# Attention's transposes and value sums in runs of two query blocks, and another bank for the eighth merged product

## The chip, the cores and the metric

The kernel runs on one core of a Trainium2 chip. The metric is the device time of one execution in microseconds. TensorE (PE in the profile) multiplies, VectorE (DVE) and ScalarE (ACT) do elementwise work and empty the matmul banks, GpSimd (POOL) and SyncE (SP) mostly issue transfers.

## The reference

A decoder layer on a sequence of 512 tokens of width 1024, in float32. A chunkwise mLSTM (4 heads) and a sliding-window attention with sinks read one normalised input. Their outputs are merged by gates and projected, and a squared-ReLU MLP and a gated per-layer embedding follow. The two parts that matter here:

```python
# attention: 16 query heads, 4 key/value heads of width 64, window 128, query blocks of 128
logits = einsum("bnqhgd,bnkhd->bnhgqk", qb, kb) * 64**-0.5   # masked to the window
m = maximum(max(logits), sink)
pexp = exp(logits - m)
probs = pexp / (sum(pexp) + exp(sink - m))
out = einsum("bnhgqk,bnkhd->bnqhgd", probs, vb)
...
merged = sigmoid(g_a) * (y_a @ w_branch_a) + sigmoid(g_b) * (y_b @ w_branch_b)
x = x + merged @ w_out
```

## The kernel before

Most products split each float32 operand into a high and a low float32r part and sum three matmuls (high-high, high-low, low-high; `pairs`, run by `chain` at L176). Such matmuls fill nearly the whole execution. The kernel is written with a tile framework: a scheduler at compile time puts each engine's instructions into a fixed order, in which an instruction that stands earlier in the text goes first among those that are ready by its own timing. The engines then run their orders and wait for each other by semaphores.

Matmul results go to banks in three rings: `ps_g` (two banks), `ps_t` (two banks) and `ps_a` (two buffers of two banks each, the large ring). After the merges that pool is closed and another takes its place, with a ring `ps_g` of two banks and a ring of three pairs of banks (`pair`).

**Attention.** The 16 units are (kp, n, ab): kp is a pair of key/value heads, n one of four query blocks, ab the head of the pair; each unit has 4 query heads. `swa_probs` makes a unit's scores in a buffer of the large ring (L783, L784), masks them into a scratch tile (a copy L794 on ScalarE and a copy under a mask L795 on VectorE; for block 0 an addition L790), and takes the softmax there (L797 to L810). The scratch tiles come from a ring of four (`tok_scratch`, tag lm); a unit uses half of one.

After both units of a block, `swa_out` transposes their eight probability tiles into another buffer of the large ring (L820), copies them out (L822) into a tile of a ring of two (tag pT), and for n > 0 makes a second copy that is masked by `tri` (L828, same ring). Then it sums over the values by plain float32 matmuls into a bank of `ps_t`, one half of the array for each of the two heads (L841): two pairs of matmuls for block 0, four pairs for the others. The result is split into high and low parts of `yb`, one query head at a time.

The loop over the units works `LOOK` = 2 units ahead and takes one projection from the list `fill` in most turns: the remaining query projections `q_proj` and the mLSTM's `qk_proj`, each 24 matmuls into a bank of `ps_g`. After the loop come `qk_proj(7)`, the mLSTM and `branch_b`, which multiplies `yb`.

**Merging.** `merge(i)`, i = 0 to 7, multiplies `ya` by a slice of `w_branch_a` into a bank of `ps_g`, and VectorE empties that bank by the product with the gate (L1026), then adds the other branch (L1027) and the result is split (tag mg). `merge_sums` makes sums of an even and an odd slice (L1045 to L1048) and splits them (tag ms). `out_proj` follows: its first product `X` takes both banks of the new `ps_g`, in reversed order, and uses the even merges only (`F11`); ScalarE copies `X` to `q1` (L1150) and then `X` is added to by the product with `F12`. Weights are cast to a high part by ScalarE and a low part by VectorE (L137, L138), four buffers of each.

Of the kernel before, what the change touches and what calls it, by code (L numbers as in the profile page):

```python
# [10 lines left out]
F32 = mybir.dt.float32  # L11
# [5 lines left out]
P = 128  # L17
# [3 lines left out]
KT = D // P  # L21
# [15 lines left out]
def block_kernel(  # L37
# [30 lines left out]
    V, A, G, T = nc.vector, nc.scalar, nc.gpsimd, nc.tensor  # L68
# [13 lines left out]
    sp = pool(st_s, "sp", side="right")  # L82
# [4 lines left out]
    def nm(s):  # L87
        n_names[0] += 1
        return f"{s}_{n_names[0]}"


    def ps_g():
        return pp.tile([P, 512], F32, tag="g", bufs=2, name=nm("psg"))

    def ps_t():
        return pp.tile([P, 512], F32, tag="t", bufs=2, name=nm("pst"))
# [15 lines left out]
    def act_hl(n="s"):  # L112
        return [act_r(n), act_r(n)]
# [9 lines left out]
    def tok_scratch(n="lm"):  # L123
        return sp.tile([P, D], F32, tag="lm", bufs=LMB, name=nm(n))
# [9 lines left out]
    def split(dst, src, scale=None):  # L134

        if scale is None:
            A.copy(dst[0], src)  # L137
            last_low[0] = V.tensor_sub(dst[1], src, r32(dst[0]))  # L138
        else:
            done = A.activation(dst[0], src, AF.Copy, scale=scale)  # L140
            V.scalar_tensor_tensor(dst[1], src, scale, r32(dst[0]), ALU.mult, ALU.subtract)
            return done
# [64 lines left out]
    ident = cp.tile([P, P], F32, name="ident")  # L207
# [107 lines left out]
    e1, _ = early_part(1)  # L315
# [75 lines left out]
    with tc.issue_after(copied.ins):  # L391
        xn2, _ = norm(2)
# [3 lines left out]
    for m in range(NT):  # L396
        if m == 1:
            columns(2, xn2)
        elif m == 2:
            with tc.issue_after(on_scalar):  # L400
                xn, _ = norm(3)
            _, on_vector = columns(3, xn)

        ps = ps_g()
        for c in range(3):
            mm_tok(ps[:, :264], wv[c], hT[K3[c]], m, first=c == 0, last=c == 2)
        t = sp.tile([P, 256], F32, tag="vs", bufs=4, name=nm("vs"))
# [57 lines left out]
    for i in range(2):  # L465
        ps = ps_t()
# [305 lines left out]

    yb = [None] * 8
    units = [(kp, n, ab) for kp in range(2) for n in range(NT) for ab in range(2)]
    probs = {}

    def swa_probs(kp, n, ab):
        k0 = max(n - 1, 0) * P
        ls = ps_a()
        for g in range(4):  # L780
            q = qs[kp * 4 + g, ab]
            o = ls[:, g * 256 : (g + 1) * 256]
            T.matmul(o, q[:, n * P : (n + 1) * P], kk[kp][ab][:, k0 : k0 + 256], start=True, stop=False)  # L783
            T.matmul(o, q[:, n * P : (n + 1) * P], kl[kp][ab][:, k0 : k0 + 256], start=False, stop=True)  # L784
        kv = 2 * kp + ab
        sk = sink[:, kv * 4 : kv * 4 + 4]
        ls3 = ls.rearrange("p (g k) -> p g k", g=4)
        lm3 = tok_scratch()[:, :512].rearrange("p (g k) -> p g k", g=4)
        if n == 0:
            V.tensor_tensor(lm3, ls3[:, :, :P], later_key.unsqueeze(1).broadcast_to([P, 4, P]), ALU.add)  # L790
        else:


            A.copy(lm3, ls3[:, :, P:])  # L794
            V.copy_predicated(lm3, later_key.bitcast(mybir.dt.int32).unsqueeze(1).broadcast_to([P, 4, P]), ls3[:, :, :P])  # L795
        mx = small("mx", 4)
        V.tensor_reduce(mx, lm3, AX.X, ALU.max, negate=True)  # L797
        nmx = small("nmx", 4)
        V.scalar_tensor_tensor(nmx, mx, 0.125, nsink[:, kv * 4 : kv * 4 + 4], ALU.mult, ALU.min)  # L799
        ds = small("ds", 4)  # L800
        V.tensor_add(ds, sk, nmx)
        es = small("es", 4)
        A.activation(es, ds, AF.Exp)
        sm = small("sm", 4)
        for g in range(4):
            A.activation(lm3[:, g, :], lm3[:, g, :], AF.Exp, bias=nmx[:, g : g + 1], scale=0.125, accum_out=sm[:, g : g + 1])  # L806
        V.tensor_add(sm, sm, es)
        rc = small("rc", 4)
        V.reciprocal(rc, sm)  # L809
        V.tensor_tensor(lm3, lm3, rc.unsqueeze(2).broadcast_to([P, 4, P]), ALU.mult)  # L810
        probs[kp, n, ab] = lm3

    def swa_out(kp, n):

        lm3 = [probs.pop((kp, n, ab)) for ab in range(2)]
        pt = ps_a()
        for ab in range(2):
            for g in range(4):
                c = ab * 512 + g * P
                T.transpose(pt[:, c : c + P], lm3[ab][:, g, :], ident)  # L820
        pT = sp.tile([P, 1024], F32, tag="pT", bufs=2, name=nm("pT"))
        A.copy(pT, pt)  # L822
        terms = [(vs[max(n - 1, 0)], pT)]
        if n:


            own = sp.tile([P, 1024], F32, tag="pT", bufs=2, name=nm("pT"))
            V.scalar_tensor_tensor(  # L828
                own.rearrange("p (g k) -> p g k", g=8),
                tri.unsqueeze(1).broadcast_to([P, 8, P]),  # L830
                0.0,
                pt.rearrange("p (g k) -> p g k", g=8),
                ALU.is_ge,
                ALU.mult,
            )
            terms.insert(0, (vd[n], own))
        o = ps_t()
        for j, (v, w) in enumerate(terms):
            for ab in range(2):
                c = (2 * kp + ab) * 64  # L840
                T.matmul(o[HALF[ab], :], v[:, c : c + 64], w[:, ab * 512 : (ab + 1) * 512], start=j == 0, stop=j == len(terms) - 1)  # L841
        for g in range(4):
            if n == 0:
                yb[kp * 4 + g] = act_hl("yb")
            split([t[:, n * P : (n + 1) * P] for t in yb[kp * 4 + g]], o[:, g * P : (g + 1) * P])

    nsink = c1.tile([P, 16], F32, name="nsink")
    with tc.issue_after(gate_in.ins):
# [11 lines left out]
    for u in range(16):  # L860
        if u % 3 or u < 3:
            fill.pop(0)()
        if u + LOOK < 16:
            swa_probs(*units[u + LOOK])
        if u % 2:
            swa_out(*units[u][:2])

    ya_parts, ya = big_hl("ya")

# [150 lines left out]
    F11, F12, F22, G1, G2, G3, G4 = ([] for _ in range(7))  # L1020

    def merge(i):
        ps = ps_g()
        mm_T(ps, load_w(w_a[i], KT * P, KT), ya)
        sg = act_f("sga")
        V.tensor_mul(sg, ps, gate_of(gad, i))  # L1026
        V.tensor_add(sg, sg, t2[i])  # L1027
        if i % 2 == 0:
            t = act_r("mg")
            own = [t[:, :256], t[:, 256:]]  # L1030
            split(own, sg[:, 256:])
            F11.append(own)
        else:
            own = act_hl("mg")
            split(own, sg)
            F22.append([q[:, :256] for q in own])
            F12.append([q[:, 256:] for q in own])
        return sg
# [80 lines left out]
    def out_proj():  # L1119

        b11, b12, b21, b22 = b_out
        X = [ps_g(), ps_g()][::-1]
        Y, Z = [[t[:, 0, :], t[:, 1, :]] for t in (pair(), pair())]

        def form(raw):
            return load_w(None, 1024, 2, raw)

        def half(ps, f, w, kh, first, last):
            for t in range(2):
                ops = []  # L1130
                for k in range(2):
                    ops += pairs([h[:, t * P : (t + 1) * P] for h in f[2 * kh + k]], [h[:, k, :] for h in w])
                chain(ps[t], ops, first and kh == 0, last and kh == 1, True)

        def prod(ps, f, b, first, last):
            for kh in range(2):
                half(ps, f, form(b[kh]), kh, first, last)

        def part_of(r, c, t):
            return xk[t + (2 if r == 1 else 0)][:, (c - 1) * 512 : c * 512]  # L1140

        def acc(ps, r, c):
            for t in range(2):
                o = part_of(r, c, t)
                V.tensor_add(o, ps[t], o)

        prod(X, F11, b11, True, False)
        q1 = [act_f("q1") for _ in range(2)]
        for t in range(2):
            copied = A.copy(q1[t], X[t])  # L1150
        with tc.issue_after(copied.ins):
            later()
        for r, c in ((2, 1), (2, 2), (1, 2)):
            for t in range(2):
                nc.gpsimd.dma_start(out=part_of(r, c, t), in_=q1[t], accum_op=ALU.add)
        for kh in range(2):
            V.tensor_add(b11[kh], b12[kh], b11[kh])
        prod(X, F12, b21, False, True)
        acc(X, 1, 1)
        with tc.issue_after(last_mm[0].ins):  # L1160
            prod(Z, G2, b11, True, False)
        acc(Z, 2, 1)
        prod(Y, G3, b12, True, False)
        acc(Y, 2, 2)
        for kh in range(2):
            V.tensor_sub(b21[kh], b21[kh], b11[kh])
            V.tensor_sub(b11[kh], b22[kh], b11[kh])
        prod(Z, G1, b11, False, False)
        acc(Z, 2, 2)
        prod(Y, F22, b21, False, True)  # L1170
        acc(Y, 2, 1)
        half(Z, G4, form(b22[0]), 0, False, False)
        two_columns_of(x1, 0, gmlp)
        two_columns_of(x1, 2, gmlp)
        half(Z, G4, form(b22[1]), 1, False, True)
        acc(Z, 1, 2)
# [386 lines left out]
```

## Time and profile before

| | us |
|---|---|
| median of 3 runs | 873.77 (873.5 to 874.34) |
| the profiled execution | 873.36 |
| its span, first to last instruction | 871.3 |
| TensorE busy with matmuls | 860.2 |
| VectorE busy | 664.8 |
| ScalarE busy | 497.0 |
| attention, first scores to first `branch_b` | 222.3 to 327.6 |

Times in the profile are counted from the start of the span. In a row of the timeline stand the start, the duration (merged rows: from the first start to the last end), the engine, the source line, the operation, the tile that is written and those that are read, the shapes, the count, and in brackets the idle time of the engine before the row and what ended it. Matmuls are pipelined: their durations overlap, and the distance from one start to the next is what each costs. In a row of the waits stand the waiting engine, tile and line, the one waited for, and the sum, the count and the longest wait. In a row of the windows stand the stretch and its length, then the busy times of PE, weight loads (PEld), DVE, ACT and POOL with counts, the granted clock of TensorE, the share of DMA and GB/s.

### The profile page before, as it was taken

The numbers are of one execution on the slowest core, as the hardware profiler recorded it, in microseconds if no ns is written. First come the engines' busy times: TensorE is split into PE (matmuls) and PEld (weight loads), VectorE is DVE, ScalarE is ACT, GpSimd is POOL, SyncE is SP. The second block draws the span as 40 slices with busy tenths as digits, with TensorE's granted clock in tenths as the row PEclk, the third lists the DMA queues.
The fourth block names the chain that finished last, engine by engine and source line by source line (L and its number), as shares of the span: only waits on it lengthen the run. The fifth ranks groups of instructions, "written<-read, shape, count | busy, mean of one in ns | idle before, by whom it ended". The sixth has DMA issues, their size and how long they took to land.

```text
span 871.3 us, 11752 instructions
## 1 busy us (share of the span) xinstructions
PE 860.2 (99%) x4422; PEld 724.9 (83%) x4422; DVE 664.8 (76%) x978; ACT 497.0 (57%) x845; POOL 51.1 (6%) x81
## 2 busy tenths in 40 slices
PE   9999999999999999999999999999999999999996
PEld 7888789999877768888878888888888888888886
DVE  7898978774698889767896669746965795688657
ACT  6776657554676667863343565345535533564743
POOL 3221111000000000000020000000000000002000
PEclk9999999999999999999999999999999999999998
DMA  8677235435121256665243711530262044206502
GB/s 299 200 193 278 97 122 206 160 135 201 50 97 43 80 199 214 219 237 191 78 72 129 258 49 37 206 121 25 75 215 97 1 142 173 73 25 135 180 1 97
DMA packets 36234, 117.76 MB, mean 135 GB/s; under 512 B 5069, under 2 KB 5069, under 8 KB 36178
## 3 DMA queue, kind: packets, MB, share of 16 engines
q1 hardware_dynamic: 28578, 95.77, 31.4%
q0 software_dynamic: 7456, 20.98, 8.7%
q8 instruction: 34, 0.56, 0.2%
q10 hardware_dynamic: 144, 0.26, 0.1%
q14 instruction: 22, 0.18, 0.1%
HBM read 99.17 MB, written 11.54 MB: 127 GB/s over the span
## 4 chain that ended last, share of the span: by engine, by line
PE 92%; DVE 3%; ACT 2%; issue 1%; DMA 1%; SPq 0%; DVEq 0%; ACTq 0%
PE psg L176 49%; PE psp L176 23%; PE psa L176 10%; PE pst L176 3%; PE pst L841 1%; PE psp L1111 1%; DMA xt<-in_x 1%; ACT lm L806 1%; ACT wh L137 1%; PE psa L783 1%; PE psa L923 1%; PE psa L945 1%; PE psa L943 1%; PE psa L944 1%; PE psa L784 1%
## 5 line engine op out<-in xcount | busy, mean ns | idle before, releaser
L137 ACT CAST wh<-wr 128x1024 fp32r<-128x1024 f32 x129 | 135.8, 1053 | 157.2 <-PE psg L176 61.0
L138 DVE TENSOR_TENSOR wl<-wr,wh 128x1024 fp32r<-128x1024 f32 x129 | 157.3, 1221 | 82.8 <-ACT wh L137 80.5
L176 PE MATMUL psg<-x,wh 128*128 128x512 f32 x512 | 157.7, 390 | 0.0
L176 PE MATMUL psp<-wh,uf 128*128 128x512 f32 x448 | 138.7, 389 | 0.0
L176 PEld LDWEIGHTS psg<-x,wh 128*128 128x128 f32 x512 | 96.1, 188 | 19.8
L176 PE MATMUL psg<-x,wl 128*128 128x512 f32 x256 | 99.7, 389 | 0.0
L176 PEld LDWEIGHTS psp<-wh,uf 128*128 128x128 f32 x448 | 84.1, 188 | 17.3
L176 PE MATMUL psp<-wl,uf 128*128 128x512 f32 x224 | 87.2, 389 | 0.0
L176 PE MATMUL psg<-h,wh 128*128 128x512 f32 x256 | 81.0, 395 | 0.7 <-DVE rc L809 0.7
L137 ACT CAST wh<-wd 128x1024 fp32r<-128x1024 f32 x44 | 46.2, 1052 | 54.2 <-PE psp L176 21.9
L138 DVE TENSOR_TENSOR wl<-wd,wh 128x1024 fp32r<-128x1024 f32 x44 | 53.2, 1220 | 14.6 <-ACT wh L137 14.5
L176 PEld LDWEIGHTS psg<-x,wl 128*128 128x128 f32 x256 | 48.1, 188 | 10.0
L176 PEld LDWEIGHTS psg<-h,wh 128*128 128x128 f32 x256 | 46.9, 188 | 11.1 <-issue 1.6
L176 PE MATMUL psg<-h,wl 128*128 128x512 f32 x128 | 50.6, 395 | 0.0
L138 DVE TENSOR_TENSOR uf<-F,uf 128x1792 fp32r<-128x1792 f32 (+2 forms) x20 | 33.0, 1652 | 21.8 <-ACT uf L137 21.8
L176 PEld LDWEIGHTS psp<-wl,uf 128*128 128x128 f32 x224 | 42.1, 188 | 8.9
L176 PE MATMUL psg<-yb,wh 128*128 128x512 f32 x128 | 40.2, 393 | 0.0
L1279 DVE SCALAR_TENSOR_TENSOR xk<-psp,r,xk 128x512 f32<-128x512 f32 x48 | 33.8, 746 | 8.0 <-PE psp L176 7.7
L176 PE MATMUL psg<-ya,wh 128*128 128x512 f32 x128 | 39.8, 391 | 0.0
L137 ACT CAST uf<-F 128x1792 fp32r<-128x1792 f32 (+2 forms) x20 | 27.9, 1395 | 20.5 <-DVE F L1255 20.4
L806 ACT ACTIVATE lm<-lm,nmx 128x128 f32<-128x128 f32 x64 | 24.9, 391 | 12.2 <-DVE nmx L799 12.2
L176 PEld LDWEIGHTS psg<-h,wl 128*128 128x128 f32 x128 | 24.0, 188 | 9.0 <-issue 4.1
(365 smaller groups left out, 1854.9 us busy)
## 6 DMA issues: line engine op xcount, KB each, us to landing
wr<-in_w_up SPq DMA_DIRECT2D x32, 512.0 KB, 3.3
wd<-in_w_down SPq DMA_DIRECT2D x24, 512.0 KB, 3.9
wr<-in_w_qsw SPq DMA_DIRECT2D x8, 512.0 KB, 4.3
gd<-gr POOLq DMA_DIRECT2D x8, 512.0 KB, 3.6
wr<-in_w_qkml SPq DMA_DIRECT2D x8, 512.0 KB, 3.2
wr<-in_w_b SPq DMA_DIRECT2D x8, 512.0 KB, 3.2
wh<-in_w_b POOLq DMA_DIRECT2D x8, 512.0 KB, 3.7
gl<-gd SPq DMA_DIRECT2D x8, 512.0 KB, 3.3
```

What stands on the lines that cost most here:

```text
L137: A.copy(dst[0], src)
L138: last_low[0] = V.tensor_sub(dst[1], src, r32(dst[0]))
L176: last_mm[0] = T.matmul(ps, l, r, start=first and i == 0, stop=last and i == len(ops) - 1, skip_group_check=parts)
L783: T.matmul(o, q[:, n * P : (n + 1) * P], kk[kp][ab][:, k0 : k0 + 256], start=True, stop=False)
L784: T.matmul(o, q[:, n * P : (n + 1) * P], kl[kp][ab][:, k0 : k0 + 256], start=False, stop=True)
L806: A.activation(lm3[:, g, :], lm3[:, g, :], AF.Exp, bias=nmx[:, g : g + 1], scale=0.125, accum_out=sm[:, g : g + 1])
L841: T.matmul(o[HALF[ab], :], v[:, c : c + 64], w[:, ab * 512 : (ab + 1) * 512], start=j == 0, stop=j == len(terms) - 1)
L923: T.matmul(psc[s], l, r, start=j == 0, stop=j == 2, skip_group_check=True)
L943: T.matmul(o, hi, vm[s][:, h, :], start=s == 0, stop=False, skip_group_check=True)
L944: T.matmul(o[:, :DV], hi, low[:, s, :], start=False, stop=False, skip_group_check=True)
L945: last_mm[0] = T.matmul(o, lo, vm[s][:, h, :], start=False, stop=s == t, skip_group_check=True)
L1279: V.scalar_tensor_tensor(o, ps[:, t, :], r2[:, 2 * toks + t : 2 * toks + t + 1], o, ALU.mult, ALU.add)
```

## The change

In attention, the two units of a block now write the two halves of one scratch tile. `swa_out` runs after every fourth unit, for two query blocks: `swa_turn` transposes a block and copies the transposes back into that same tile, and makes the masked copy as before, for both blocks; then `swa_sum` makes the value sums of both, the later block first; then both are split. The tiles of tag pT now hold the masked copies alone. The eighth merge writes a bank of `ps_t` instead of `ps_g`, and `out_proj` takes its two banks for `X` in the order of the ring.

```diff
+        if ab == 0:
+            block[kp, n] = tok_scratch()
-        lm3 = tok_scratch()[:, :512].rearrange("p (g k) -> p g k", g=4)
+        lm3 = block[kp, n][:, ab * 512 : (ab + 1) * 512].rearrange("p (g k) -> p g k", g=4)
...
-    def swa_out(kp, n):
-        lm3 = [probs.pop((kp, n, ab)) for ab in range(2)]
+    def swa_turn(kp, n):
+        pT = block.pop((kp, n))
         pt = ps_a()
-        for ab in range(2):
-            for g in range(4):
-                c = ab * 512 + g * P
-                T.transpose(pt[:, c : c + P], lm3[ab][:, g, :], ident)
-        pT = sp.tile([P, 1024], F32, tag="pT", bufs=2, name=nm("pT"))
+        for c in range(0, 1024, P):
+            T.transpose(pt[:, c : c + P], pT[:, c : c + P], ident)
         A.copy(pT, pt)
...
+        return terms
+
+    def swa_out(kp, ns):
+        terms = {n: swa_turn(kp, n) for n in ns}
+        sums = {n: swa_sum(kp, terms[n]) for n in reversed(ns)}
+        for n in ns:
+            for g in range(4):
+                if n == 0:
+                    yb[kp * 4 + g] = act_hl("yb")
+                split([t[:, n * P : (n + 1) * P] for t in yb[kp * 4 + g]], sums[n][:, g * P : (g + 1) * P])
+
+    def swa_sum(kp, terms):
         o = ps_t()
         for j, (v, w) in enumerate(terms):
             for ab in range(2):
                 c = (2 * kp + ab) * 64
                 T.matmul(o[HALF[ab], :], v[:, c : c + 64], w[:, ab * 512 : (ab + 1) * 512], start=j == 0, stop=j == len(terms) - 1)
+        return o
...
-        if u % 2:
-            swa_out(*units[u][:2])
+        if u % 4 == 3:
+            kp, n, _ = units[u]
+            swa_out(kp, (n - 1, n))
...
     def merge(i):
-        ps = ps_g()
+        ps = ps_t() if i == KT - 1 else ps_g()
...
-        X = [ps_g(), ps_g()][::-1]
+        X = [ps_g(), ps_g()]
```

More of the change, by code (lines that the diff above doesn't have):

```diff
@@ L774, in block_kernel @@
     units = [(kp, n, ab) for kp in range(2) for n in range(NT) for ab in range(2)]
-    probs = {}
+    block = {}
     def swa_probs(kp, n, ab):
@@ L810, in swa_probs @@
         V.tensor_tensor(lm3, lm3, rc.unsqueeze(2).broadcast_to([P, 4, P]), ALU.mult)
-        probs[kp, n, ab] = lm3
-    def swa_out(kp, n):
-        lm3 = [probs.pop((kp, n, ab)) for ab in range(2)]
+    def swa_turn(kp, n):
+        pT = block.pop((kp, n))
         pt = ps_a()
-        for ab in range(2):
-            for g in range(4):
-                c = ab * 512 + g * P
-                T.transpose(pt[:, c : c + P], lm3[ab][:, g, :], ident)
-        pT = sp.tile([P, 1024], F32, tag="pT", bufs=2, name=nm("pT"))
+        for c in range(0, 1024, P):
+            T.transpose(pt[:, c : c + P], pT[:, c : c + P], ident)
         A.copy(pT, pt)
@@ L841, in swa_out @@
                 T.matmul(o[HALF[ab], :], v[:, c : c + 64], w[:, ab * 512 : (ab + 1) * 512], start=j == 0, stop=j == len(terms) - 1)
[L842 to L845, printed above, removed]
+        return o
     nsink = c1.tile([P, 16], F32, name="nsink")
```

## The prediction

> **What bounds the kernel now.** I read the page first (span, busy shares, chain), then the waits of TensorE's matmul queue, then the two stages that the change touches in order of time.
>
> ```profile
> span 871.3 us, 11752 instructions
> PE 860.2 (99%) x4422; PEld 724.9 (83%) x4422; DVE 664.8 (76%) x978; ACT 497.0 (57%) x845; POOL 51.1 (6%) x81
> PE 92%; DVE 3%; ACT 2%; issue 1%; DMA 1%; SPq 0%; DVEq 0%; ACTq 0%
> PE psg L176 <- DVE sga L1026: 0.9, 1, 0.9
> PE psg L176 <- DVE rc L809: 0.7, 1, 0.7
> PE psa L783 <- DVE lm L795: 0.5, 1, 0.5
> PE pst L841 <- ACT pT L822: 0.2, 1, 0.2
> 222.00:327.60 105.60, 104.33 (x540) 79.05 (x539) 87.86 (x192) 71.03 (x232) 1.59 (x3) 1.00 0.28 94
> ```
>
> TensorE is busy 99% of the span and is 92% of the chain. In the list of its waits these four are all after the start of the kernel. Three lie in attention, which runs from 222 to 327.6 us with 104.33 of 105.60 us busy (last row, first busy column; the last 1.00 before the DMA share is the granted clock). So the time falls only by what TensorE no longer waits, or no longer spends between instructions.
>
> **Part 1: joining runs of value sums (L841).** A value sum is a plain float32 matmul on half the array (128*64); its neighbours are 128*128. A run of one block, from the projection around it:
>
> ```profile
> 251.53 0.62 PE L176 MATMUL psg<-h,wh 128*128 128x512 f32 x2
> 252.08 1.08 PE L841 MATMUL pst<-pT,vd 128*64 128x512 f32 x4
> 252.99 1.03 PE L841 MATMUL pst<-pT,vs 128*64 128x512 f32 x4
> 253.95 0.51 PE L176 MATMUL psg<-h,wl 128*128 128x512 f32 x1
> 254.29 0.40 PE L176 MATMUL psg<-h,wh 128*128 128x512 f32 x1
> L841 PE MATMUL pst<-pT,vs x40: 592/592/644, 241.8 to 325.5; 128*64 128x512 f32 x40
> ```
>
> A projection matmul advances TensorE by 0.23 (two take 0.62, one 0.39). From 251.53 to 254.29 are 2.76 us. Three projections in it take 0.69, so eight sum matmuls take 2.07. They run in pairs, one per half: the second group lasts 1.03, of which the last matmul is 0.59 (tile row), so a pair advances by about 0.43, four by 1.72. The other 0.35 is the price of entering and leaving the run: the next projection is late, and itself takes 0.51 instead of 0.39 with the following one 0.34 later. Eight runs pay it, one per query block. The change has the two sums of a pair of blocks traced back to back. Each join saves 0.35; four joins 1.40, none 0.
>
> I take two joins, 0.70. The second block's sum must be ready when the first one ends, else the scheduler puts projections between. The first needs 0.86 (block 0, two pairs) or 1.72 (four pairs). What separates the two blocks shows here, after the scores of units 4 and 5:
>
> ```profile
> 247.70 0.73 DVE L795 COPY_PREDICATED lm<-later_key,psa 128x512 f32<-128x512 int32 x1
> 250.02 0.73 DVE L795 COPY_PREDICATED lm<-later_key,psa 128x512 f32<-128x512 int32 x1
> 250.71 1.21 DVE L828 SCALAR_TENSOR_TENSOR pT<-tri,psa 128x1024 f32<-128x1024 f32 x1
> 248.57 1.04 PE L820 MATMUL psa<-ident,lm 128*128 128x128 f32 x8
> 249.36 0.71 PE L176 MATMUL psg<-h,wh 128*128 128x512 f32 x2
> 249.91 0.40 PE L176 MATMUL psg<-h,wl 128*128 128x512 f32 x1
> 249.64 1.02 ACT L822 COPY pT<-psa 128x1024 f32<-128x1024 f32 x1 [0.99 <-PE psa L820]
> ```
>
> The large ring has two buffers, and a mask copy on VectorE frees one for the next transposes: the copy of 247.70 ended at 248.43 and the transposes began at 248.57. The second copy came 2.3 us later. Two blocks of a pair take the two buffers so freed, each then needs 1.02 on ScalarE and, from block 1 on, 1.21 on VectorE. So the lag is 1 to 2.3 us: more than 0.86, about equal to 1.72. Hence the pairs with blocks 2 and 3 join and those with 0 and 1 do not.
>
> **Part 2: joining runs of transposes (L820).** From 248.57 to 249.91 are 1.34 us for eight transposes and two projections (0.46): 0.110 per transpose. A run of sixteen elsewhere (L1111):
>
> ```profile
> 477.79 1.91 PE L1111 MATMUL psp<-ident,xk 128*128 128x128 f32 x16
> 479.46 0.48 PE L176 MATMUL psp<-wh,ms 128*128 128x512 f32 x1
> 479.77 0.39 PE L176 MATMUL psp<-wl,ms 128*128 128x512 f32 x1
> 477.70:479.50 1.80, 1.80 (x19) 1.71 (x17) 0.43 (x1) 1.51 (x2) 0.00 (x0) 1.00 0.46 139
> ```
>
> 477.79 to 479.77 less one projection is 1.75, or 0.109 per transpose. Joining transposes saves nothing. The Trainium skill, TensorE: Matmul & The Clock Gate, section Part 4: PE-mode transpose, says that transposes do not count as activity for the clock gate, which would make longer runs dangerous. The row of the run of sixteen shows a granted clock of 1.00. Were it halved, a run would last 3.50 instead of 1.75, and the four of the change 7.0 more than I forecast, 878.9: I give that 1 in 100, within the chance of slower.
>
> **Part 3: the tiles.** The shared tile replaces 16 allocations in the ring of four by 8, each held until its sum ends; the copied transposes return into it, so the two pT buffers serve only the products with tri. Copies, products, splits and exponentials keep number and size. The even block's step moves behind a further projection and score product; its 8 transposes, copy, product, sums and 8 split instructions pass work on PE, ACT and DVE. It issues no DMA, so on SP and POOL only weight loads are passed, ahead of use. I cost this at nothing: the projections in between (24 matmuls, 5.4 us each) hide it, and at the end qk_proj(7) does. If they ran out, one product of 1.21 would show per pair.
>
> **Part 4: a score product that waited.**
>
> ```profile
> 265.32 0.39 PE L176 MATMUL psg<-h,wh 128*128 128x512 f32 x1
> 266.18 0.39 PE L783 MATMUL psa<-kk,qs 128*128 128x256 f32 x1 [0.47 <-DVE lm L795]
> 266.40 0.28 PE L784 MATMUL psa<-kl,qs 128*128 128x256 f32 x1
> ```
>
> The transposes of block 2 had one buffer and the scores of unit 7 the other, so unit 8 stood until the mask copy was done: 0.86 between starts instead of 0.23, and 0.22 instead of 0.12 for the next, 0.73 in all. Behind the change the transposes come two units later and unit 8 finds a buffer free: minus 0.73. Four new places appear where the second block's transposes follow a score product at once. I charge one of them with 0.63, at a chance of one in four: plus 0.16. Bounds: none, or all four, 2.5. The other waits of attention (0.65, 0.16) I leave where they are.
>
> **Part 5: the eighth merge.**
>
> ```profile
> 441.04 0.39 PE L176 MATMUL psg<-ya,wl 128*128 128x512 f32 x1
> 442.31 0.47 PE L176 MATMUL psg<-wh,mg 128*128 128x512 f32 x1 [0.88 <-DVE sga L1026]
> 442.61 0.39 PE L176 MATMUL psg<-wl,mg 128*128 128x512 f32 x1
> 438.68 0.68 DVE L1026 TENSOR_TENSOR sga<-psg,gl 128x512 f32<-128x512 f32 x1
> 441.47 0.69 DVE L1026 TENSOR_TENSOR sga<-psg,gl 128x512 f32<-128x512 f32 x1 [0.37 <-PE psg L176]
> 445.42 0.41 DVE L1046 TENSOR_TENSOR ms<-ms,sga 128x256 f32<-128x256 f32 x1
> 446.34 0.62 ACT L137 CAST ms<-ms 128x512 fp32r<-128x512 f32 x1
> 446.86 0.58 ACT L1150 COPY q<-psg 128x512 f32<-128x512 f32 x1
> ```
>
> The last merge ends at 441.04, the first product of w_out (X) starts at 442.31, 1.04 late, and its successor 0.08 late: 1.12. It waited for the product that empties merge 7's bank (441.47 to 442.16). Merge 6's bank was emptied at 439.36. With merge 7 in the other ring, both banks of X are free at 441.27; X's first half uses only merges 0 and 2. What is late next: after 24 matmuls, at 441.27 + 24 x 0.227 = 446.72, the next product adds into X[0], which ScalarE must have copied (L1150). That copy stands on ScalarE's queue behind the cast of ms, which waits for VectorE's sum at 445.42 to 445.83, and that chain starts with merge 7's product, whose time does not move. Cast 445.9 to 446.5, copy to 447.0, a weight load of 0.19: 447.24 instead of 446.72, 0.52 lost again. I take 1.12 - 0.52 = 0.60. Ends: 0 and 1.12.
>
> **Sum:** -0.70 - 0.73 + 0.16 - 0.60 = -1.87 us. The profiled execution took 873.36 (span 871.3), 0.41 under the median of 873.77. On it the sum gives 871.49, on the median 871.90.
>
> **The rivals.**
> - *Everything lands*: four joins, no new wait, ScalarE's copy ahead of the cast: -1.40 - 0.73 - 1.12 = -3.25, 870.5. For it: sums are traced with the later block first, so the earlier one may be held until both are ready.
> - *The bank does not matter*: X waits for all of the closed pool, or the copy takes everything back: -1.27, 872.5. The row names merge 7's product but not its bank.
> - *Attention unchanged*: no run joins, the wait of 266 comes back elsewhere; only the merge: -0.60, 873.2. For it: the 2.3 us lag.
> - *Slower*: both large buffers hold transposes at once, and the next scores, fixed in TensorE's order, stand behind the second product with tri. VectorE has little room:
>
> ```profile
> 300.00:313.00 13.00, 12.35 (x68) 9.32 (x67) 12.30 (x29) 8.01 (x28) 0.53 (x1) 1.00 0.38 127
> ```
>
> It is busy 12.30 of 13.00 us here (third busy column). One 1.21 at each of four pairs is 4.84; with 0.70 and 0.60 kept and 0.73 lost, +3.5: 877.3. It passes the bound from (1.75 + 1.30) / 4 = 0.76 per pair. Against it: projections are there to fill, and four waits of that kind do not stand in the trace of before. The Trainium skill (the same page, section Part 2: What happens when you issue a matmul) says that matmuls keep program order; at 266.18 nothing else ran, which agrees.
>
> **How the numbers follow.** A difference under 0.2%, 1.75 us, cannot be told from none. Forecast 0.38 (871.9; own range 870.9 to 872.8), everything 0.17, bank 0.15, attention unchanged 0.18, slower 0.12. Faster is the second and three quarters of the first: 0.46. Slower 0.12. The rest, 0.42, is the same. The range of 869.9 to 874.6 takes in the forecast, the first three rivals, the remaining waits of attention at its low end and two new ones of 0.63 at its high end, and leaves out most of the last rival.
>
> **What would show it.** Right: four to six runs of L841 instead of eight, some of 12 or 16; transposes still 0.109 each; no row that waits near 266; the first X product 0.23 behind the last merge and a short wait about 5.5 us later. Wrong: eight separate runs, a wait of the first X product on L1026, or new waits on L795 or L828 before L783 and L820.

## The result and the profile after

The changed kernel took 871.25 us in the median of 7 runs (870.70 to 871.76), the kernel before 874.02 us in 7 runs beside them (873.5 to 875.38). The ratio is 0.9966, with a 95% interval of 0.9954 to 0.9978: a gain of 2.8 us, of which the interval leaves 1.9 to 4.0. Five more runs on another occasion gave 871.48 against 874.29, ratio 0.9964 (0.9951 to 0.9978). The forecast was 871.9 us.

The profiled execution of the changed kernel took 870.98 us. The first lines of its page, and then the whole list of TensorE's waits of 0.2 us and more (the sum, the count, the longest):

```profile
span 869.0 us, 11746 instructions
PE 859.4 (99%) x4422; PEld 725.1 (83%) x4422; DVE 664.2 (76%) x978; ACT 496.6 (57%) x845; POOL 51.0 (6%) x81
```

```profile
PE psg L278 <- DVE zero L216: 1.1, 1, 1.1
PE pst L354 <- ACT sd L324: 0.9, 1, 0.9
PE psg L176 <- ACT q L1160: 0.2, 1, 0.2
```

TensorE is busy 859.4 of 869.0 us. The four waits that the list of before had after the start of the kernel (0.9, 0.7, 0.5 and 0.2) are gone, and one of 0.2 is new, on ScalarE's copy of `X` (L1150 of before is L1160 here, L1026 is L1036, L841 is L853, L820 is L819).

To see where the time went, the traces are cut at the starts of five matmuls: first scores, first and last product with `ya`, first product of `X` and first product with `G2`. The rows that set the cuts, in the timeline of TensorE, before (its last merge and first `X` stand in the prediction) and after:

```profile
222.34 0.28 PE L783 MATMUL psa<-kk,qs 128*128 128x256 f32 x1
...
397.07 0.71 PE L176 MATMUL psg<-ya,wh 128*128 128x512 f32 x2
...
453.31 0.39 PE L176 MATMUL psp<-wh,ms 128*128 128x512 f32 x1
```

```profile
223.03 0.28 PE L783 MATMUL psa<-kk,qs 128*128 128x256 f32 x1
...
395.36 0.71 PE L176 MATMUL psg<-ya,wh 128*128 128x512 f32 x2
...
439.34 0.39 PE L176 MATMUL pst<-ya,wl 128*128 128x512 f32 x1
439.56 0.39 PE L176 MATMUL psg<-wh,mg 128*128 128x512 f32 x1
...
450.97 0.39 PE L176 MATMUL psp<-wh,ms 128*128 128x512 f32 x1
```

| stage, us | before | after | difference |
|---|---|---|---|
| up to the first scores | 222.34 | 223.03 | +0.69 |
| attention and mLSTM, first scores to first `ya` | 174.73 | 172.33 | -2.40 |
| merges, first to last `ya` | 43.97 | 43.97 | 0 |
| last `ya` to first `X` | 1.26 | 0.23 | -1.03 |
| first `X` to first `G2` | 11.00 | 11.41 | +0.41 |
| from there to the last matmul | 410.60 | 410.61 | +0.01 |

The sum is -2.32, and the spans differ by 2.3. The +0.69 does not come from an edited instruction: the same 1342 matmuls stand ahead of the first scores in both, and nearly all of the shift (0.64) is there by 37 us, in waits for the first normalised rows. Without it the profiled pair shows -3.02. In the kernels shown here, which all run the same instructions ahead of the first scores, that start lies between 222.34 and 223.87. Two traces of the changed kernel have 223.03 and 223.09, and two of `copy_first` 223.64 and 223.71, so whether it goes by the execution or by the program stays open. Below, kernels are compared by stages first and by totals second.

**Attention.** There are four runs of value sums instead of eight, of 12, 16, 12 and 16 matmuls. One of 12:

```profile
303.28 0.61 PE L176 MATMUL psg<-h,wh 128*128 128x512 f32 x2
303.83 1.08 PE L853 MATMUL pst<-pT,vd 128*64 128x512 f32 x4
304.74 1.89 PE L853 MATMUL pst<-lm,vs 128*64 128x512 f32 x8
306.56 0.50 PE L176 MATMUL psg<-h,wl 128*128 128x512 f32 x1
306.89 0.63 PE L176 MATMUL psg<-h,wh 128*128 128x512 f32 x2
```

The later block's four matmuls with `vd` come first, then its four with `vs`, then the earlier block's four. From 303.28 to 306.89 are 3.61; three projections take 0.69 and six pairs 2.58 at the prediction's 0.43, which leaves 0.34, the price of one run where two were paid before. That the earlier block's sum was held for the later one shows in the first pair:

```profile
249.30 1.93 ACT L820 COPY lm<-psa 128x1024 f32<-128x1024 f32 x2 [0.73 <-PE psa L819]
254.28 1.89 PE L853 MATMUL pst<-lm,vs 128*64 128x512 f32 x8
```

The first of the two copies, all that block 0's sum needs, ends at 250.31, and that sum is the second half of the row of eight, from 255.14. In the four pairs the earlier block's sum starts 4.0 to 6.5 us after its tiles are ready, and the later block's tiles are ready 1.9 to 4.4 us after the earlier one's.

A run of sixteen transposes in TensorE's timeline:

```profile
247.60 0.39 PE L176 MATMUL psg<-h,wh 128*128 128x512 f32 x1
248.11 1.97 PE L819 MATMUL psa<-ident,lm 128*128 128x128 f32 x16
249.83 0.49 PE L176 MATMUL psg<-h,wh 128*128 128x512 f32 x1
250.16 0.39 PE L176 MATMUL psg<-h,wl 128*128 128x512 f32 x1
```

The window around it:

```profile
248.00:249.90 1.90, 1.79 (x17) 1.79 (x17) 1.84 (x4) 1.17 (x2) 0.00 (x0) 1.00 0.04 9
```

From 248.11 to 250.16, less one projection of 0.23, are 1.82, or 0.114 each: joining saved nothing, and the granted clock stayed at 1.00 (the figure before the DMA share). It is the only run of sixteen. In the other three pairs projections stand between the transposes: 8 and 8 (from 271.18 and 272.86), 8 and 8 (297.11 and 300.07), 12 and 4 (314.69 and 318.80). TensorE's busy time in attention, before and after:

```profile
222.00:328.00 106.00, 104.73 (x541) 79.39 (x540) 88.15 (x193) 71.35 (x233) 1.59 (x3) 1.00 0.28 95
```

```profile
222.00:328.00 106.00, 105.82 (x552) 81.80 (x551) 90.84 (x196) 74.95 (x238) 2.12 (x4) 1.00 0.29 98
```

TensorE sat idle 1.27 us before and 0.18 after. With four joins of 0.35 that accounts for -1.40 - 1.09 = -2.49, against the -2.40 of the stage. Idle time is less than what a wait costs, though. Counted by starts (how much later than without a wait the next matmuls begin), the three waits of before, at 241.85, 266.18 and 301.18, cost about 0.2, 0.73 and 0.9, 1.8 in all. In the changed kernel some matmuls start late with hardly any idle time: the sixteen transposes (248.11 is 0.51 behind 247.60 instead of 0.23, and the second of them 0.17 behind the first instead of 0.11: 0.34), the sums at 253.37 (0.1), the scores at 265.77 (0.2) and the transposes at 272.86 (0.17), 0.8 in all. So the waits gave -1.8 + 0.8 = -1.0 by starts, and with the joins -2.4. The wait near 266 (0.47 idle) is gone, and so is one that I had left in place, 0.65 idle behind the transposes at 299.5 of before. At that place the changed kernel has:

```profile
300.07 1.04 PE L819 MATMUL psa<-ident,lm 128*128 128x128 f32 x8
300.86 0.36 PE L783 MATMUL psa<-kk,qs 128*128 128x256 f32 x1
...
301.90 0.63 PE L176 MATMUL psg<-h,wh 128*128 128x512 f32 x2
```

The eight score matmuls of a unit now stand between the transposes and the next projection, which starts at 301.90 without waiting.

**Merging.** TensorE's timeline of the changed kernel at the second product into `X`:

```profile
444.78 0.39 PE L176 MATMUL psg<-wh,mg 128*128 128x512 f32 x1
445.38 0.50 PE L176 MATMUL psg<-wh,mg 128*128 128x512 f32 x1 [0.22 <-ACT q L1160]
445.72 0.39 PE L176 MATMUL psg<-wl,mg 128*128 128x512 f32 x1
```

ScalarE's timeline there:

```profile
444.22 0.62 ACT L137 CAST ms<-ms 128x512 fp32r<-128x512 f32 x1 [0.63 <-DVE ms L1056]
444.75 1.09 ACT L1160 COPY q<-psg 128x512 f32<-128x512 f32 x2
```

The first product of `X` starts 0.22 behind the last merge. After 5.8 us the next product waits for the copy of `X`, which stands behind the cast of `ms`: 445.38 comes 0.60 after 444.78 instead of 0.23, and the next matmul 0.11 late, 0.48 in all.

### The profile page after: what moved, and what is told of

It is laid out like the page before. It is cut to its first block, busy times and chain, and to the rows that moved or that the text cites. A ratio compares the mean times of both kernels' runs of the same rounds, so it can differ in the third digit from the quotient of the medians.

```text
span 869.0 us, 11746 instructions
## 1 busy us (share of the span) xinstructions
PE 859.4 (99%) x4422; PEld 725.1 (83%) x4422; DVE 664.2 (76%) x978; ACT 496.6 (57%) x845; POOL 51.0 (6%) x81
## 4 chain that ended last, share of the span: by engine, by line
PE 86%; issue 7%; DVE 3%; ACT 2%; DMA 1%; SPq 0%; POOL 0%; POOLq 0%; ACTq 0%; DVEq 0%
PE psg L176 44%; PE psp L176 23%; PE psa L176 10%; PE pst L176 4%; PE psp L1121 1%; DMA xt<-in_x 1%; PE pst L853 1%; PE psa L783 1%; PE psa L784 1%; ACT wh L137 0%; DVE wl L138 0%; ACT lm L808 0%; DMA wh<-in_w_b 0%; PE psa L933 0%; PE psa L953 0%
## 5 line engine op out<-in xcount | busy, mean ns | idle before, releaser
L176 PE MATMUL psg<-ya,wh 128*128 128x512 f32 x112 | 34.9, 391 | 0.0
```

Source lines behind the costliest of these rows:

```text
L176: last_mm[0] = T.matmul(ps, l, r, start=first and i == 0, stop=last and i == len(ops) - 1, skip_group_check=parts)
```

## The experiments

The theory: three things add up. The sums of each pair of blocks run as one, because they are traced with the later block first (1.40); attention's waits shrink with the new order (about 1.0); the eighth merge's bank frees `X` (1.03), of which the late copy takes some 0.4 back. Rivals: the shared tile is what brings the gain in attention; the joined transposes bring it; the order of `X`'s tiles, not the bank, frees its first product. Except where a diff says so, an edit starts from the changed kernel. The first four edits ran beside 874.09 of before (27 runs), the four of the last rows are single runs beside a single 873.58, and the changed kernel and copy_first ran once more beside 874.29 (9 runs).

| kernel | us | ratio to before | attention | to first `X` | `X` to `G2` |
|---|---|---|---|---|---|
| before | 874.02 | 1 | 174.73 | 1.26 | 11.00 |
| after | 871.25 | 0.9966 (0.9954 to 0.9978) | 172.33 | 0.23 | 11.41 |
| attn_only | 872.18 | 0.9980 (0.9971 to 0.9990) | 172.25 | 1.26 | 10.96 |
| merge_only | 873.39 | 0.9995 (0.9986 to 1.0005) | 174.83 | 0.23 | 11.41 |
| earlier_first | 873.03 | 0.9988 (0.9979 to 0.9998) | 173.89 | 0.23 | 11.41 |
| copy_first | 870.86 | 0.9970 (0.9958 to 0.9982) | 172.60 | 0.23 | 10.88 |
| after, again | 871.48 | 0.9964 (0.9951 to 0.9978) | 172.28 | 0.23 | 11.39 |
| copy_first, again | 871.05 | 0.9954 (0.9941 to 0.9966) | 172.49 | 0.23 | 10.88 |
| order_only | 874.24 | single run | 174.93 | 1.26 | 10.98 |
| bank_only | 873.45 | single run | 174.79 | 0.23 | 11.41 |
| single_blocks | 873.46 | single run | 174.96 | 0.23 | 11.39 |
| turns_single | 873.26 | single run | 174.84 | 0.23 | 11.41 |

Three kernels with the attention of before (merge_only, order_only, bank_only) put that stage at 174.79 to 174.93, 0.06 to 0.20 above the trace of before, and the five traces with the attention of the changed kernel (after and copy_first, twice each, and attn_only) lie between 172.25 and 172.60: differences under 0.4 in that column say nothing. The stage that the table leaves out, first to last `ya`, took 43.93 to 43.97, but 44.24 in attn_only, 44.80 in merge_only and 45.03 in earlier_first. Their edits do not explain it: the changed kernel has the merges of earlier_first, and before those of attn_only.

**attn_only** and **merge_only**: each half of the change by itself.

```diff
-        ps = ps_t() if i == KT - 1 else ps_g()
+        ps = ps_g()
...
-        X = [ps_g(), ps_g()]
+        X = [ps_g(), ps_g()][::-1]
```

> Only the attention part of the change; the eighth merge stays in the small ring of before and X keeps its reversed order. Theory A (two independent parts): the stage from the first scores to the first product with ya takes 172.3 us as in the changed kernel (174.7 before), the gap between the last merge and X is 1.26 again, and the whole is about 2.4 us faster than before. Rival B (the parts help each other, or the later stages give the gain back): the stage is shorter but the whole gains under 1.5 us.

The other half is the same two lines the other way round, on the kernel before.

> Only the merge part: the eighth merge in the other ring and X in the ring's order, attention as before. Theory A: the gap from the last merge to X falls from 1.26 to 0.23 us, then X's second product waits 0.4 to 0.5 for ScalarE's copy of X, net 0.6 us faster than before. Rival B: the copy takes everything back, 0.0; rival C: no wait for the copy, 1.1 faster.

attn_only took 872.18 (10 runs) against 874.09: -1.91 in the totals, -2.48 in its stage. The interval of attn_only leaves 0.9 to 2.5, in which both its theory and rival B lie; the stages, 172.25 and 1.26, are those of theory A. merge_only took 873.39 (10 runs), -0.70, and its interval includes no change; by stages it has -1.03 and +0.41, -0.62. In these stages the halves do not touch each other, and the two totals add up to -2.61, beside -2.77 for the whole change. What the merge half brings is shown by its stages; the total alone would not show it.

**earlier_first**: the sums traced in the order of the blocks.

```diff
-        sums = {n: swa_sum(kp, terms[n]) for n in reversed(ns)}
+        sums = {n: swa_sum(kp, terms[n]) for n in ns}
```

> The changed kernel with one word less: the sums of a pair of blocks are traced earlier block first. Everything else, tiles too, is as in the changed kernel. By theory A (what joins the runs is that the earlier block's sum has to follow the later one's into the ring of banks) there are eight runs of sums again, each new run costs 0.35 us on TensorE, and the kernel is 1.4 us slower than the changed one, about 1.4 faster than before. By rival B (a run costs nothing, the gain is all from waits that went) the time stays within 0.3 us of the changed kernel.

There are eight runs of sums again. The first two, in TensorE's timeline:

```profile
251.20 1.08 PE L853 MATMUL pst<-lm,vs 128*64 128x512 f32 x4
252.21 0.50 PE L176 MATMUL psg<-h,wl 128*128 128x512 f32 x1
...
253.93 0.61 PE L176 MATMUL psg<-h,wh 128*128 128x512 f32 x2
254.47 1.08 PE L853 MATMUL pst<-pT,vd 128*64 128x512 f32 x4
```

Its window of attention:

```profile
222.00:328.00 106.00, 105.64 (x544) 79.82 (x544) 87.93 (x191) 70.13 (x231) 1.59 (x3) 1.00 0.28 92
```

Block 0's sum runs as soon as it can, at 251.20, and block 1's is not ready when it ends: projections come between, up to 254.47. That gap of 3.3 us between the starts is the lag of the prediction at work, longer than the 1 to 2.3 that I had read from the trace of before, and it keeps the runs apart. In the other pairs the starts lie 2.3, 3.8 and 2.8 apart, with one, fifteen and three matmuls between the sums. With the later block first, block 0's sum is held until block 1's has started. The stage is 1.56 longer than in the changed kernel. Idle time in the window is 0.36 instead of 0.18, so four prices of 0.35 and 0.18 of waiting make 1.58. So the order in which the two sums are traced is worth 1.4 in joins. Here the transposes still come two blocks at a step and the sums do not join, and TensorE is idle only 0.36: the waits of before went with the place of the transposes, not with the joins. The total, 1.06 under before, is less sure than the stage: its runs spread from 871.56 to 874.81. That the earlier block's sum is held, ready as it is, is seen in the changed kernel; here the sum that is traced second is the one that is ready late, which does not test it. How the scheduler holds a sum no run shows.

**single_blocks**: the shared tile stays, each block is turned and summed by itself as before.

```diff
-        if u % 4 == 3:
+        if u % 2:
...
-            swa_out(kp, (n - 1, n))
+            swa_out(kp, (n,))
```

> The changed kernel, with the step of transposes and sums after every second unit again, for one block; the shared tile and the copy back into it stay. Theory A (joined runs give 1.40 of attention's 2.40, the rest is waits that went because the scores of the next unit no longer stand behind a block's transposes): the stage from the first scores to the first product with ya takes 174.0 to 174.8 us, with eight runs and the waits of before near 266 and 300. Rival B (the longer-lived shared tile relieves the ring of scratch tiles, and the waits go by that): eight runs, but 173.7 or less and no wait near 266.

Attention takes 174.96, as long as before within what that column can tell and 0.16 above theory A's range. The eight runs and the two longer waits are back, which rules out rival B:

```profile
PE psg L176 <- DVE rc L811: 0.7, 1, 0.7
PE psa L783 <- DVE lm L797: 0.5, 1, 0.5
```

The tile by itself brings nothing and costs nothing that can be measured.

**turns_single**: transposes and copies per block as before, sums by pairs.

```diff
+        kp, n, _ = units[u]
+        if u % 2:
+            turned_block[kp, n] = swa_turn(kp, n)
         if u % 4 == 3:
-            kp, n, _ = units[u]
             swa_out(kp, (n - 1, n))
...
-        terms = {n: swa_turn(kp, n) for n in ns}
+        terms = {n: turned_block.pop((kp, n)) for n in ns}
```

> The changed kernel with the transposes and the copies of each block after its two units, as before, and only the sums in pairs. Theory A (a run of transposes costs nothing to enter, so only the sums need joining): four runs of sums, and the attention stage within 0.5 us of the changed kernel's 172.3 unless a wait like that of before near 266 comes back, which would add 0.7. Rival B (joining the transposes matters as such): each transpose run split adds about 0.35, four of them 1.4.

The sums are in four runs, and yet the stage takes 174.84: all of the gain is lost, 2.5 us, where theory A had at most 1.2 and rival B 1.4. The window of attention:

```profile
222.00:328.00 106.00, 103.69 (x542) 79.95 (x540) 89.12 (x193) 73.58 (x231) 2.12 (x4) 1.00 0.29 94
```

Rows of TensorE's timeline that start late:

```profile
265.83 0.40 PE L176 MATMUL psg<-h,wl 128*128 128x512 f32 x1
266.38 0.39 PE L783 MATMUL psa<-kk,qs 128*128 128x256 f32 x1
...
317.54 0.70 PE L176 MATMUL psg<-h,wh 128*128 128x512 f32 x2 [0.69 <-DVE sm L809]
...
324.73 1.08 PE L855 MATMUL pst<-pT,vs 128*64 128x512 f32 x4 [1.01 <-DVE pT L826]
```

VectorE's timeline, the product that the last one waited for:

```profile
323.47 1.21 DVE L826 SCALAR_TENSOR_TENSOR pT<-tri,psa 128x1024 f32<-128x1024 f32 x1
```

TensorE sat idle 2.31 us in the window, 1.04 more than before and 2.13 more than in the changed kernel. The last run of sums waits 1.01 for the product with `tri`, which VectorE starts at 323.47; in the changed kernel that product starts at 321.23 and nothing waits. By idle time and joins the stage should stand at 174.73 + 1.04 - 1.40 = 174.37, 0.47 short of what it takes. By starts it comes out: the three rows above cost 0.4, 0.9 and 1.1 (the score product of 266.38 starts 0.55 behind its forerunner instead of 0.23, with 0.15 of idle time), three late starts at 248.19, 252.68 and 273.26 another 0.9, together 3.3 beside 1.8 before. That is +1.5, the joins are -1.4, and the sum is the measured +0.1. So transposing two blocks at one step saves nothing per transpose, but the order that comes with it has few waits, and here going without it costs 2.5, more than the runs of sums bring. Whether another order would be as good with single transposes was not tried.

**order_only** and **bank_only**: the two lines of the merge half apart, each on the kernel before.

```diff
-        X = [ps_g(), ps_g()][::-1]
+        X = [ps_g(), ps_g()]
```

> The kernel before, with X taking its two banks in the ring's order; the eighth merge stays in the small ring. Theory A (X waited because its first tile stood on merge 7's bank, its second on merge 6's): the gap from the last merge to X falls from 1.26 to 0.23 us without the other ring, and from X's start to the product with G2 it takes 11.4 us as in the merge part alone. Rival B (X waits for all that the closed pool held): the gap stays at 1.26.

```diff
-        ps = ps_g()
+        ps = ps_t() if i == KT - 1 else ps_g()
```

> The kernel before, with the eighth merge in the other ring and X still in reversed order. Theory A (a bank free early for each tile of X is enough, in either order): gap 0.23 us. Rival B (X waits for the closed pool): 1.26. Rival C (the new banks of X are those of the other ring): 1.26 as well, and order_only 0.23.

The last merge and the first product of `X`, in order_only and in bank_only:

```profile
442.24 0.39 PE L176 MATMUL psg<-ya,wl 128*128 128x512 f32 x1
443.50 0.47 PE L176 MATMUL psg<-wh,mg 128*128 128x512 f32 x1 [0.88 <-DVE sga L1026]
```

```profile
442.04 0.39 PE L176 MATMUL pst<-ya,wl 128*128 128x512 f32 x1
442.27 0.39 PE L176 MATMUL psg<-wh,mg 128*128 128x512 f32 x1
```

The order does nothing, against theory A of order_only, and the bank does all of it. bank_only also shows that `X` doesn't wait for its whole closed pool, since the `ps_t` bank of merge 7 belongs to that pool too. Why the first product waits for merge 7's bank in both orders stays open: both may put that bank first, or the new ring may wait for the old ring as a whole.

**copy_first**: both splits of the last `merge_sums` stand behind the two copies of `X` on ScalarE's queue.

```diff
-        parts((G1, G2), sa)
-        return lambda: parts((G3, G4), sb)
+        first, second = lambda: parts((G1, G2), sa), lambda: parts((G3, G4), sb)
+        return first, second
...
-            later()
+            for part in later:
+                part()
```

> The changed kernel, with both splits of the last merge sums put behind ScalarE's copies of X, so that the copy no longer stands behind the cast of ms. By theory A (the copy of X is late because of that cast) the wait of 0.48 us in X's second product goes and nothing else moves: 0.4 to 0.5 us faster than the changed kernel, 870.8. By rival B (the copy is late for another reason, or the split of ms that is now later is waited for by the product with G2) it is the same or slower.

TensorE's timeline at the product that waited in the changed kernel:

```profile
446.75 0.39 PE L176 MATMUL psg<-wl,mg 128*128 128x512 f32 x1
446.98 0.39 PE L176 MATMUL psg<-wh,mg 128*128 128x512 f32 x1
```

ScalarE's timeline beside it, the second copy of `X` and the cast:

```profile
446.10 0.59 ACT L1161 COPY q<-psg 128x512 f32<-128x512 f32 x1 [0.77 <-PE psg L176]
446.58 0.62 ACT L137 CAST ms<-ms 128x512 fp32r<-128x512 f32 x1
```

Each copy now starts as soon as its half of `X` is ready, the cast follows, and no matmul waits. `X` to `G2` falls from 11.41 to 10.88, which is 0.53, the prediction's price of the late copy (0.52). Its total was 870.86 (6 runs), which beside its own runs of before is a ratio of 0.9970, no better than the changed kernel's 0.9966. The two kernels were then run side by side:

> The changed kernel itself, beside the variant with the copies first, on one chip. Both theories expect the ratio that it had, 0.9966, or 871.2 us against 874.1, with a first product of X 0.23 us behind the last merge and 11.41 us from there to the first product of G2.

> The changed kernel with both splits of the last merge sums behind the two copies of X on ScalarE's queue. If the wait of X's second product for its copy is a real cost of the path, its 0.53 us (11.41 to 10.88 from the first product of X to the first of G2, in the profile taken before) come off the total: 870.7 against 871.2 of the changed kernel, ratio 0.9960. Rival: the late splits hold up the products with G1 to G4 in some executions, and the total is that of the changed kernel.

The changed kernel took 871.48 (5 runs), copy_first 871.05 (5 runs) against 874.29: ratios 0.9964 (0.9951 to 0.9978) and 0.9954 (0.9941 to 0.9966). `X` to `G2` was again 11.39 and 10.88. Side by side it was 0.4 us ahead in the median, but the intervals overlap, and its two traced executions were no shorter than those of the changed kernel (spans of 869.3 beside 869.0 both times): the first scores came 0.6 later, and attention took 0.2 to 0.3 longer. The 0.5 us of the stage is shown twice; a faster total is not shown.

## Why the prediction came out

The forecast was 871.9 us and the time 871.25, or 871.48 on the other occasion; the sum of the terms was -1.87 where the stages show -3.0 and the medians -2.8. It was right in its sign and in the merge, and too small in attention, in two terms that both erred to the same side; no error made up for another.

- *Part 1, joined sums: -0.70, measured -1.40.* The price of a run was right: 0.34 in the run of 12 above. The step that failed is the count of joins, two where all four came: I let the lag between the two blocks decide. The lag is there, and longer than I read it (1.9 to 4.4 us between the blocks' tiles in the changed kernel, where I had 1 to 2.3), but it decides only if the earlier block's sum goes first, as in earlier_first, where no pair joined. The rival "everything lands" named the right reason, and I gave it too little weight.
- *Part 2, joined transposes: 0.* Right as a price: 0.114 each in the run of sixteen beside 0.110 in eight. Only one pair of four has such a run, though. The rule of the Trainium skill (TensorE: Matmul & The Clock Gate, Part 4: PE-mode transpose) that transposes do not count for the clock gate cost nothing here: 1.00 was granted around the run. But turns_single shows that the waits hang on when the transposes come.
- *Part 3, the shared tile: 0.* Right: single_blocks takes as long as before. The cover that I named held in the changed kernel; in turns_single it ran out at the last block, for 1.01 idle, near the 1.21 that I had priced.
- *Part 4, the wait near 266: -0.73, with +0.16 for a new one.* That wait went. The step "the other waits of attention I leave where they are" failed: the waits of 0.65 and 0.16 went too, another 1.1 by starts. No new wait reached the 0.2 us of the list, but by starts the new ones cost 0.8, not 0.16; 0.34 of it are transposes that wait for a mask copy (L797, at 248.11), close to what I had charged. In all the waits gave -1.0 where I had -0.57.
- *Part 5, the eighth merge: -0.60, measured -0.62.* Both terms were right: 1.03 off the gap beside 1.04 predicted, and 0.48 of waiting for the late copy beside 0.52 (its last steps, 447.0 and 0.19, add to 447.19 and not to 447.24, which makes it 0.47). In copy_first that wait is gone. The new order of `X`'s tiles does nothing.
- *The slower rival* did not come: TensorE was idle 0.18 us in attention, and none of the new late starts there costs more than 0.34. *Attention unchanged* is excluded by attn_only, and *the bank does not matter* by bank_only.

The profiled execution's start, 0.69 later than before's, hid a quarter of the gain in that pair. In the trace of earlier_first the first scores came 1.53 later than before's, and the stage of the merges took 1.06 longer, neither of which its edit touches; these waits stand there:

```profile
PE pst L354 <- DVE xn L341: 1.5, 1, 1.5
PE psa L994 <- DVE ya L141: 1.0, 1, 1.0
```

## What to carry to other kernels

Where a short run of matmuls in another array shape pays a fixed price, join runs. Here tracing the part that is ready last first made sure of the join, and the lag between the parts cost nothing, because other work filled it. When a bound engine starts its next product earlier, read the queue of the engine that must empty the bank: here nearly half of what the freed bank brought went to a copy that stood behind a cast. For gains of a few tenths of a per cent, cut the trace into stages at named instructions: the time up to the first scores alone differed by 1.5 us between the traces here, which is half of the change. And count what a wait costs from start to start: the wait of 0.47 idle near 266 cost 0.73.

## What was not expected of the hardware

The price of a run of 128*64 sums among 128*128 products hardly depends on its length: 0.35 for 8 matmuls (251.53 to 254.29 of before) and 0.34 for 12 (303.28 to 306.89). Read the same way, the run of 4 at 290.08 of before gives 0.37 and the run of 16 at 322.78 of the changed kernel 0.35. The sums differ from the projections in shape and also in being plain float32 and not float32r; no run separates the two. The Trainium skill (TensorEngine Tiling (Array Packing), Key Properties) says that a change of tiling mode drains TensorE; a price per run, whatever its length, agrees with it. The transposes keep the shape 128*128 and pay no such price in runs of 8 or 16.
